# Conditioning rows of a hybrid decoder layer loaded as a stream of half rows, with the row rate set by stage

## The chip, the cores and the metric

The kernel runs on one core of a Trainium2 chip, as one program. The metric is the device time of one execution in microseconds (us). A core has TensorE (PE in the profile: matrix products into eight PSUM banks), VectorE (DVE), ScalarE (ACT), GpSimd (POOL) and SyncE (SP). SP does nothing here but issue DMA transfers, one after the other; each issue waits until the tile that it fills is free, and what stands behind it in SP's queue waits too.

## The reference, cut to what matters

One decoder layer on x (512 tokens by 2048), all in fp32. A conditioning vector c gives six modulation vectors of 2048 each, by a 2048 by 12288 matrix (100 MB, the largest input):

```python
c_act = jax.nn.silu(c)
mod = (c_act @ w_ada + b_ada).reshape(B, 6, D)
sh1, sc1, gt1, sh2, sc2, gt2 = [mod[:, j][:, None, :] for j in range(6)]

h = rmsnorm(x, g_norm_mix) * (1.0 + sc1) + sh1
q, k, v, xr, xg = split(h @ w_in)
o_attn = stick_breaking_attention(q, k, v)                 # 8 heads of 128
hr = rg_lru(causal_depthwise_conv(xr, w_conv, b_conv), ...)  # width 1024
o_lru = hr * gelu(xg)
mixed = concat([rmsnorm(o_attn, g_attn_out), rmsnorm(o_lru, g_lru_out)])
x = x + gt1 * (mixed @ w_out)

h = rmsnorm(x, g_norm_mlp) * (1.0 + sc2) + sh2
x = x + gt2 * (square(relu(h @ w_mlp_in)) @ w_mlp_out)
return rmsnorm(x, g_norm_final)
```

## The kernel before, in words

Tokens lie along the free axis, channels on the 128 partitions, so x is 16 blocks of 128 by 512. Every product is made three times: each operand is split into a rounded high part (ACT, a copy to fp32r) and the remainder (DVE, `low`, line 112), and `mm3` (lines 217 to 223) issues high x high, high x low, low x high.

A **row** of w_ada is the 2048 weights of 128 modulation values: 128 partitions by 2048, 1 MB. `ada` loads it in two halves of 512 KB into tiles with the tag `x` and multiplies each on DVE by the broadcast silu(c) (`cb`), which also sums along the row (line 178, STT below); line 185 adds the two sums and the bias. There are 96 rows, 16 for each of SC1, SH1, GT1, SC2, SH2 and GT2. GT2 has code of its own in the MLP, which the change leaves alone.

The work before the MLP, in the order of PE:

- **Phase 1** (the loop at `for k in range(NK)`): 16 steps of 24 products of 512 columns make the recurrence input xr from w_in and the *unnormalized* x times (1 + sc1) times the gain. Step k needs x block k, row k of SC1 (`prep1`) and 512 KB of w_in. The sum of squares of x runs beside it; a POOL all-reduce and six small operations (`rnorm`) turn it into r1.
- **Phase 2**: 16 steps for the first two heads' q and k and four heads' v. Step k needs row k of SH1 and the normalized block k (`prep2`: t = x r1, high and remainder of t + sh1).
- **q and k of heads 2 to 7, v of heads 4 to 7, xg**: `qk_group(2)`, `v_group(4)`, `qk_group(4)`, `qk_group(6)`, `xg_group(0)`, `xg_group(4)`, 16 steps (ticks) of 12 products each. Attention (`pair`), the recurrence (`conv`, `gates`, `scans`) and the rows of GT1, SC2, SH2 (`adas`) are put between them by lanes: a lane yields a number of ticks to wait before its next piece. For rows that number is `pace[0]`.
- **Out product**: 48 ticks of w_out, rows beside them at pace 1.58 and 1.42, until SH2 is done (`ensure`).

Loads of weights go into `wr` tiles (four of them) at raised priority; `later` pins an instruction to the place in its queue where the code has it. Pools: `x` had three tiles of 1024 columns, `tt` five of 1280 (temporaries of attention, and of the squares in phase 1).

## Time and profile before

| | |
|---|---|
| time, median of 3 runs | 2094.67 us (2091.67 to 2095.12) |
| the profiled execution, its own time | 2092.94 us |
| its span, first to last instruction | 2091.2 us |
| PE busy | 2016.1 us, 96% of the span |
| DVE busy | 1765.3 us, 84% |
| ACT busy | 1084.4 us, 52% |
| DMA | 441.46 MB, mean 211 GB/s |

A matrix product's busy time overlaps the next one's, so 96% is not a measure of how close PE is to its best; stages are compared by how long they take for the same number of products. Rows in the views have the start in us, the duration, engine, line, operation and tiles, and in brackets the idle time of the engine before it and what ended it. A line of waits gives the total, the number and the longest.

### The profile page before, as it was taken

Reading aid. Unit: us, or ns where it says so; the run is one execution under the profiler, and the core shown is the slowest. Engines: PE = TensorE matmul, PEld = TensorE weight load, DVE = VectorE, ACT = ScalarE, POOL = GpSimd, SP = SyncE. Lnnn points to the kernel's source line nnn. Section 1 sums busy time; section 2 is a strip of 40 time slices with the busy share of each in tenths; the row PEclk is TensorE's granted clock in tenths of the full one; section 3 lists DMA queues with packets and bytes.
Section 4 is the critical chain, followed back from the end, with each engine's and each line's share of the span. In section 5 each row is a group of like instructions: output and inputs, shape, how many; then the busy total and the mean of one; then the engine's idle time right before and its main releaser. Section 6 shows DMA issues by size and latency. Waiting matters only on the chain.

```text
span 2091.2 us, 38025 instructions
## 1 busy us (share of the span) xinstructions
PE 2016.1 (96%) x14532; PEld 1892.5 (90%) x14532; DVE 1765.3 (84%) x2993; ACT 1084.4 (52%) x1580; POOL 179.5 (9%) x282
## 2 busy tenths in 40 slices
PE   7989999999999898999999999999999999999997
PEld 5779898778777798999999999999999999999996
DVE  6898875878887679999999999999879778777986
ACT  4433564786432367555555545556435555555542
POOL 0000000000000000111211211200010210210000
PEclk9999999999999999999999999999999999999999
DMA  8887744535679743665655655655577667567744
GB/s 293 288 289 240 221 152 136 181 126 177 223 241 315 267 147 111 215 195 188 215 187 172 217 185 172 228 169 205 194 249 264 223 242 272 203 243 258 249 146 147
DMA packets 205625, 441.46 MB, mean 211 GB/s; under 512 B 20353, under 2 KB 41985, under 8 KB 205442
## 3 DMA queue, kind: packets, MB, share of 16 engines
q1 hardware_dynamic: 178642, 360.78, 52.2%
q0 software_dynamic: 21760, 71.32, 9.2%
q10 hardware_dynamic: 5040, 6.93, 1.0%
q8 instruction: 114, 1.87, 0.4%
q14 instruction: 69, 0.57, 0.1%
HBM read 375.25 MB, written 63.70 MB: 210 GB/s over the span
## 4 chain that ended last, share of the span: by engine, by line
PE 49%; DVE 3%; DMA 2%; issue 1%; ACT 0%; SPq 0%; DVEq 0%; ACTq 0%
PE ps_mm L1004 8%; PE ps_mm L1003 8%; PE ps_mm L1005 8%; PE ps_z L1004 6%; PE ps_z L1003 6%; PE ps_z L1005 6%; PE ps_o L1005 2%; PE ps_o L1004 2%; PE ps_o L1003 2%; DVE w L112 1%; DMA raw<-in_w_mlp_out_dram 1%; DMA a<-in_w_adaT_dram 1%; DMA a<-x 1%; DMA a<-sum 0%; DVE a L1180 0%
## 5 line engine op out<-in xcount | busy, mean ns | idle before, releaser
L1005 PE MATMUL ps_mm<-a,w 128*128 128x256 f32 x1696 | 476.6, 282 | 1.1 <-DVE w L112 1.1
L1003 PE MATMUL ps_mm<-a,w 128*128 128x256 f32 x1696 | 477.1, 282 | 0.5 <-DVE a L1016 0.5
L1004 PE MATMUL ps_mm<-a,w 128*128 128x256 f32 x1696 | 477.2, 282 | 0.0
L967 ACT ACTIVATE w<-raw 128x768 fp32r<-128x768 f32 x244 | 205.0, 841 | 330.8 <-PE ps_mm L1004 145.9
L1005 PE MATMUL ps_z<-a,w 128*128 128x256 f32 x1304 | 368.7, 283 | 7.0 <-DVE w L112 6.9
L112 DVE TENSOR_TENSOR w<-ts,w 128x1024 fp32r<-128x1024 f32 x244 | 297.7, 1220 | 89.5 <-PE ps_mm L1004 41.0
L1003 PE MATMUL ps_z<-a,w 128*128 128x256 f32 x1304 | 368.5, 283 | 0.5 <-DVE a L1019 0.5
L1004 PE MATMUL ps_z<-a,w 128*128 128x256 f32 x1304 | 368.3, 283 | 0.0
L973 ACT ACTIVATE w<-ts 128x1024 fp32r<-128x1024 f32 x244 | 258.3, 1059 | 152.1 <-DVE ts L969 134.2
L1005 PEld LDWEIGHTS ps_mm<-a,w 128*128 128x128 f32 x1696 | 319.3, 189 | 1.4 <-DVE w L112 1.4
L1003 PEld LDWEIGHTS ps_mm<-a,w 128*128 128x128 f32 x1696 | 319.4, 188 | 0.8 <-issue 0.7
L1004 PEld LDWEIGHTS ps_mm<-a,w 128*128 128x128 f32 x1696 | 319.6, 189 | 0.1
L112 DVE TENSOR_TENSOR w<-raw,w 128x768 fp32r<-128x768 f32 (+1 forms) x296 | 267.3, 904 | 42.7 <-ACT w L204 27.8
L1005 PEld LDWEIGHTS ps_z<-a,w 128*128 128x128 f32 x1304 | 246.8, 189 | 8.3 <-DVE w L112 8.2
L178 DVE SCALAR_TENSOR_TENSOR x<-x,cb 128x1024 f32<-128x1024 f32 x160 | 196.4, 1233 | 61.1 <-DMA x<-in_w_adaT_dram 60.5
L1003 PEld LDWEIGHTS ps_z<-a,w 128*128 128x128 f32 x1304 | 246.9, 189 | 0.9 <-issue 0.7
L1004 PEld LDWEIGHTS ps_z<-a,w 128*128 128x128 f32 x1304 | 246.9, 189 | 0.2 <-DVE a L112 0.2
L204 ACT ACTIVATE wh<-wr 128x512 fp32r<-128x512 f32 (+1 forms) x184 | 113.1, 618 | 171.3 <-PE ps_mm L222 74.3
L223 PE MATMUL ps_mm<-a,wl 128*128 128x512 f32 x448 | 178.0, 398 | 7.2 <-DVE wl L112 7.1
L219 PE MATMUL ps_mm<-a,wh 128*128 128x512 f32 x448 | 178.0, 397 | 4.0 <-DVE a L380 3.1
L222 PE MATMUL ps_mm<-a,wh 128*128 128x512 f32 x448 | 176.8, 395 | 0.0
L961 DVE TENSOR_TENSOR ts<-raw 128x512 f32<-128x512 f32 x244 | 166.5, 683 | 4.8 <-DMA raw<-in_w_mlp_out_dram 3.2
(326 smaller groups left out, 4087.0 us busy)
## 6 DMA issues: line engine op xcount, KB each, us to landing
x<-in_w_adaT_dram SPq DMA_DIRECT2D x160, 512.0 KB, 5.2
raw<-in_w_mlp_out_dram SPq DMA_DIRECT2D x124, 512.0 KB, 4.2
raw<-in_w_mlp_in_dram SPq DMA_DIRECT2D x120, 512.0 KB, 3.8
wr<-in_w_in_dram SPq DMA_DIRECT2D x160, 256.0 KB, 3.7
part<-a POOLq DMA_DIRECT2D x84, 256.0 KB, 3.7
a<-part SPq DMA_DIRECT2D x84, 256.0 KB, 6.1
prod<-a POOLq DMA_DIRECT2D x63, 256.0 KB, 6.2
sum<-a POOLq DMA_DIRECT2D x56, 256.0 KB, 3.7
```

The source lines that it names most:

```text
L112: tt(out=out, in0=full, in1=f32(high), op=ALU.subtract)
L178: stt(out=t, in0=t, scalar=1.0, in1=cb[q * n // 1024][:, o : o + n], op0=ALU.mult, op1=ALU.mult, accum_out=ga[:, q : q + 1],)
L204: act(h[:, :n], r[:, :n], AF.Copy)
L219: first = mm(out, wh, ah, start=start, stop=False, **kw)
L222: mm(out, wh, al, start=False, stop=False, **kw)
L223: mm(out, wl, ah, start=False, stop=stop, **kw)
L961: tt(out=t[:, : 2 * HT].rearrange("p (a b) -> p a b", a=2), in0=r[:, HT : 3 * HT].rearrange("p (a b) -> p a b", a=2), in1=r[:, q_(0)].unsq ...
L967: act(h, r[:, HT:], AF.Copy)
L973: act(h, t, AF.Copy)
L1003: mm(out, wh[:, blk(i)], ah, start=st, stop=False, **kw)
L1004: mm(out, wh[:, blk(i)], al, start=False, stop=False, **kw)
L1005: mm(out, wl[:, blk(i)], ah, start=False, stop=j == js[-1], **kw)
```

## The change

Four edits, all ahead of the MLP.

1. `ada` becomes `Rows`: a list of half rows in the order of use, `load(n, tags)` that issues the next n loads, and `row` that multiplies. In phases 1 and 2 (EARLY) the tiles come from `x` and `tt` in turn, each multiplication is followed by one more load, and a load more is made at each fourth step. GT1, SC2 and SH2 are loaded through `x` alone as they are used (MID) until `xg_group(4)`; from there five halves are loaded ahead through `x` and `tt` (LATE), each half has its own turn in the lane, and its multiplication is pinned. `x` has four tiles now, `tt` four.
2. The attention constants are made after phase 1 (`triangles`), by POOL and ACT; DVE no longer makes them at the start.
3. `prep1` splits straight from x: one ACT copy with the scale for the high part, one DVE operation for the remainder, in place of a scaled copy, a copy and a subtraction. x stays unscaled, so `prep2` multiplies by the gain as well.
4. x is loaded two blocks ahead and not three, the all-reduce is begun at step 13 and the small operations on r1 are written behind row 15; weights of step k + 1 are written ahead of step k's products. Row pace: 3.2 ticks instead of 3.5, 1.6 in the first half of `qk_group(4)`, 2.1 in the out product instead of 1.58 and 1.42.

```diff
-    "front": {"x": 3, "tt": 5, "wr": 4, "wh": 3, "wl": 3},
+    "front": {"x": 4, "tt": 4, "wr": 4, "wh": 3, "wl": 3},
...
+    class Rows:
+        def __init__(self, *ms):
+            self.todo = [(m * NK + j, q) for m in ms for j in range(NK) for q in range(2)]
+            self.tiles = {}
+        def load(self, n, tags):
...
+            for _ in range(n):
+                if self.todo and tags:
+                    i, q = self.todo.pop(0)
+                    t = T(next(tags))[:, :1024]
+                    later(queue.dma_start(t, w_adaT[i * P : (i + 1) * P, q * 1024 : (q + 1) * 1024]))
+                    self.tiles[i, q] = t
+        def row(self, m, j, tags, q=None):
...
+            for q_ in (0, 1) if q is None else (q,):
+                if (i, q_) not in self.tiles:
+                    self.load(2, tags)
+                t = self.tiles.pop((i, q_))
+                ins = stt(
+                    out=t, in0=t, scalar=1.0, in1=cb[q_], op0=ALU.mult, op1=ALU.mult, accum_out=self.ga[:, q_ : q_ + 1],
+                )
+                if q is not None:
+                    later(ins)
+                del t
+                if tags is not MID:
+                    self.load(1, tags)
...
+    rows, rows2 = Rows(SC1, SH1), Rows(GT1, SC2, SH2)
+    MID = itertools.cycle(["x"])
+    LATE = itertools.cycle(["x", "tt"])
...
-        act(xs[k], xs[k], AF.Identity, scale=g)
-        xhl[k] = split(xs[k], "a")
+        h, lo = T("a", F32R), T("a", F32R)
+        act(h, xs[k], AF.Copy, scale=g)
+        stt(out=lo, in0=xs[k], scalar=g, in1=f32(h), op0=ALU.mult, op1=ALU.subtract)
+        xhl[k] = h, lo
...
-        tt(out=t, in0=t, in1=r1, op=ALU.mult)
+        stt(out=t, in0=t, scalar=gm1[:, k : k + 1], in1=r1, op0=ALU.mult, op1=ALU.mult)
...
+    EARLY = itertools.cycle(["x", "tt"] * 3 + ["x"])
...
     for k in range(NK):
-        w = weights1(k)
...
         if k + 1 < NK:
-            prep1(k + 1)
-        if k >= NK - 2:
-            prep2(k - (NK - 2))
+            w_next = weights1(k + 1)
+            if k + 2 < NK:
+                load_x(k + 2)
+            if k + 2 == NK - 1:
+                r1_gen = rnorm_steps([acc], D, None)
+                next(r1_gen)
+            prep1(k + 1, EARLY)
+            if k + 1 == NK - 1:
+                r1 = next(r1_gen)
+            if k % 4 == 4 - 1:
+                rows.load(1, EARLY)
+        else:
+            prep2(0)
+            prep2(1)
...
+    triangles()
...
-    pace = [3.5]
+    pace = [3.2]
...
+    pace[0] = 1.6
+    def recurrence():
+        pace[0] = 3.2
...
+    tags2[0] = LATE
+    rows2.load(5, LATE)
     xg_group(4, BANKS[4:])
...
-    pace[0] = 1.58
+    pace[0] = 2.1
...
-    pace[0] = 1.42
+    pace[0] = 2.1
```

How this stands in the queues, at three places. **DVE at the start of the program**, before (`x_25` and `x_26` are the halves of SC1's row 0, `cb_1` and `cb_2` the halves of silu(c), `n_8` and `n_9` the constants):

```order
L134 MEMSET ones_64 128x128
L136 MEMSET n_8_88 128x128
L147 MEMSET eps_68 128x1
L142 CAST nones_r_66<-n_8_88 128x128
L446 TENSOR_SCALAR spl_72<-vec_63 128x8
L141 CAST ntri_65<-n_9_90 128x128
L178 SCALAR_TENSOR_TENSOR x_25_123,ga_24_122<-x_25_123,cb_1_76 128x1024
L178 SCALAR_TENSOR_TENSOR x_26_126,ga_24_122<-x_26_126,cb_2_77 128x1024
L185 SCALAR_TENSOR_TENSOR mods_69<-ga_24_122,vec_63 128x1
L317 SCALAR_TENSOR_TENSOR gm1_70<-mods_69,vec_63 128x1
```

and with the change (`x_20` and `tt_21` are the halves now):

```order
L148 MEMSET ones_64 128x128
L149 MEMSET eps_68 128x1
L492 TENSOR_SCALAR spl_72<-vec_63 128x8
L194 SCALAR_TENSOR_TENSOR x_20_108,ga_27_122<-x_20_108,cb_1_76 128x1024
L194 SCALAR_TENSOR_TENSOR tt_21_110,ga_27_122<-tt_21_110,cb_2_77 128x1024
L203 SCALAR_TENSOR_TENSOR mods_69<-ga_27_122,vec_63 128x1
L350 SCALAR_TENSOR_TENSOR gm1_70<-mods_69,vec_63 128x1
```

The constant `ntri`, which waits for POOL, stood ahead of the first row and is gone from DVE.

**DVE at the end of phase 1**, before, from SC1's row 15 (`x_222`, `x_223`) to the weights of phase 2 (`wl_265`); `n_208` and `n_209` are r1 in the making, `a_204` to `a_220` remainders of x blocks and of weights:

```order
L178 SCALAR_TENSOR_TENSOR x_222_933,ga_221_932<-x_222_933,cb_1_76 128x1024
L112 TENSOR_TENSOR a_214_894<-a_182_763,a_213_892 128x512
L178 SCALAR_TENSOR_TENSOR x_223_936,ga_221_932<-x_223_936,cb_2_77 128x1024
L289 TENSOR_SCALAR n_208_873<-n_208_873 128x512
L112 TENSOR_TENSOR a_217_923<-wr_215_920,a_216_922 128x512
L291 TENSOR_TENSOR n_208_873<-n_208_873,n_209_875 128x512
L112 TENSOR_TENSOR a_220_929<-wr_218_926,a_219_928 128x512
L292 SCALAR_TENSOR_TENSOR n_208_873<-n_208_873,n_209_875 128x512
L185 SCALAR_TENSOR_TENSOR mods_69<-ga_221_932,vec_63 128x1
L293 SCALAR_TENSOR_TENSOR n_209_875<-n_208_873,n_209_875 128x512
L317 SCALAR_TENSOR_TENSOR gm1_70<-mods_69,vec_63 128x1
L178 SCALAR_TENSOR_TENSOR x_227_947,ga_226_946<-x_227_947,cb_1_76 128x1024
L178 SCALAR_TENSOR_TENSOR x_228_950,ga_226_946<-x_228_950,cb_2_77 128x1024
L112 TENSOR_TENSOR wl_265_1072<-wr_263_1069,wh_264_1071 128x512
```

and with the change, from the square of x block 15 that the all-reduce waits for (`n_11`) to the first operation on r1 (`n_217`); `x_220` and `x_230` are halves of SH1's row 1, `tt_219` the second half of its row 0, `a_233` the remainder of x block 15:

```order
L353 SCALAR_TENSOR_TENSOR a_222_883<-a_202_812,gm1_70,a_221_882 128x512
L332 TENSOR_TENSOR n_11_99<-n_11_99,n_216_868 128x512
L194 SCALAR_TENSOR_TENSOR tt_219_875,ga_235_966<-tt_219_875,cb_2_77 128x1024
L203 SCALAR_TENSOR_TENSOR mods_69<-ga_235_966,vec_63 128x1
L194 SCALAR_TENSOR_TENSOR x_220_878,ga_240_979<-x_220_878,cb_1_76 128x1024
L112 TENSOR_TENSOR a_225_913<-wr_223_910,a_224_912 128x512
L112 TENSOR_TENSOR a_228_919<-wr_226_916,a_227_918 128x512
L353 SCALAR_TENSOR_TENSOR a_233_932<-a_215_866,gm1_70,a_232_931 128x512
L112 TENSOR_TENSOR wl_270_1066<-wr_268_1063,wh_269_1065 128x512
L112 TENSOR_TENSOR wl_273_1084<-wr_271_1081,wh_272_1083 128x512
L194 SCALAR_TENSOR_TENSOR x_230_924,ga_240_979<-x_230_924,cb_2_77 128x1024
L318 TENSOR_SCALAR n_217_871<-n_217_871 128x512
```

The operations on r1 stood between the last row, the weights' remainders and the closing of row 15; they now stand behind everything that phase 1 needs, and behind two weights of phase 2 and three halves of SH1.

**SP at the beginning of the out product**, before (`x` are half rows, `wr` weights of w_out):

```order
L196 DMA wr_1068_5290<-in_w_out_dram 128x512
L174 DMA x_1073_5317<-in_w_adaT_dram 128x1024
L174 DMA x_1074_5320<-in_w_adaT_dram 128x1024
L196 DMA wr_1075_5324<-in_w_out_dram 128x512
L196 DMA wr_1079_5346<-in_w_out_dram 128x512
L174 DMA x_1084_5369<-in_w_adaT_dram 128x1024
L196 DMA wr_1086_5376<-in_w_out_dram 128x512
L174 DMA x_1085_5372<-in_w_adaT_dram 128x1024
L196 DMA wr_1093_5406<-in_w_out_dram 128x512
L174 DMA x_1091_5399<-in_w_adaT_dram 128x1024
L174 DMA x_1092_5402<-in_w_adaT_dram 128x1024
```

and with the change:

```order
L219 DMA wr_1087_5320<-in_w_out_dram 128x512
L182 DMA x_1068_5278<-in_w_adaT_dram 128x1024
L219 DMA wr_1091_5346<-in_w_out_dram 128x512
L182 DMA tt_1073_5301<-in_w_adaT_dram 128x1024
L182 DMA x_1095_5369<-in_w_adaT_dram 128x1024
L219 DMA wr_1096_5372<-in_w_out_dram 128x512
L182 DMA tt_1101_5396<-in_w_adaT_dram 128x1024
L219 DMA wr_1102_5398<-in_w_out_dram 128x512
L182 DMA x_1106_5421<-in_w_adaT_dram 128x1024
L219 DMA wr_1107_5424<-in_w_out_dram 128x512
L219 DMA wr_1114_5455<-in_w_out_dram 128x512
```

Halves often came two next to each other; now one stands between two weights, in `x` and `tt` in turn, and five halves are loaded before the first of them is multiplied. Counted over SP's queue, the half rows are 10, 8, 20, 8 and 50 in `v_group(4)`, `qk_group(4)`, `qk_group(6)` with `xg_group(0)`, `xg_group(4)` and the out product before, and 12, 10, 25, 11 and 38 with the change. Ahead of the remainder of hT block 0 (the first operand of phase 2), DVE has 35 multiplications of half rows before and 38 with the change.

## Rows read from the trace of the kernel before

**Rows 1.** Windows by stage: busy us of each engine (count), PE clock, DMA share, GB/s.

```profile
15.77:123.51 107.74, 94.39 (x384) 73.86 (x385) 93.06 (x178) 50.82 (x86) 3.25 (x1) 0.97 0.87 299
123.51:213.97 90.46, 90.46 (x577) 81.93 (x576) 80.46 (x144) 32.74 (x52) 0.00 (x0) 1.00 0.77 257
334.86:386.58 51.72, 50.78 (x216) 40.34 (x216) 27.30 (x48) 28.33 (x47) 0.00 (x0) 1.00 0.44 139
386.58:513.23 126.65, 122.73 (x584) 101.19 (x585) 107.10 (x185) 92.70 (x139) 0.00 (x0) 1.00 0.49 158
558.20:706.95 148.75, 138.75 (x577) 106.72 (x575) 122.20 (x224) 46.00 (x77) 9.99 (x11) 1.00 0.82 280
```

**Rows 2.** Timeline of the start, ACT, DVE and PE.

```profile
7.73 1.06 ACT L153 ACTIVATE cb<-cb 128x1024 f32<-128x1024 f32 x1 [5.22 <-DMA cb<-in_c_dram]
...
10.75 0.23 DVE L141 CAST ntri<-n 128x128 fp32r<-128x128 f32 x1 [6.51 <-POOL n L138]
10.89 1.22 DVE L178 SCALAR_TENSOR_TENSOR x<-x,cb 128x1024 f32<-128x1024 f32 x1
...
15.77 0.80 PE L219 MATMUL ps_mm<-a,a 128*128 128x512 f32 x1 [7.92 <-ACT a L204]
```

**Rows 3.** Window from DVE's first half row to the first operand of phase 2.

```profile
10.85:115.10 104.25, 87.20 (x360) 68.16 (x360) 89.84 (x173) 49.51 (x84) 3.25 (x1) 0.99 0.85 293
```

**Rows 4.** Waits of DVE, 8 to 124 us.

```profile
DVE x L178 <- DMA x<-in_w_adaT_dram: 7.8, 11, 1.8
...
DVE n L301 <- ACT tt L300: 4.9, 7, 1.4
```

**Rows 5.** Groups of DVE, 10.5 to 123.5 us: busy us, mean ns of one.

```profile
L112 DVE TENSOR_TENSOR a<-a,a 128x512 fp32r<-128x512 f32 x16 | 11.0, 685 | 0.3 <-ACT a L116 0.3
...
L185 DVE SCALAR_TENSOR_TENSOR mods<-ga,vec 128x1 f32<-128x1 f32 x18 | 3.8, 213 | 0.1
```

**Rows 6.** Timeline of the end of phase 1, DVE and POOL.

```profile
98.90 3.28 DVE L178 SCALAR_TENSOR_TENSOR x<-x,cb 128x1024 f32<-128x1024 f32 x1 [0.18 <-DMA x<-in_w_adaT_dram]
...
114.31 0.75 DVE L327 SCALAR_TENSOR_TENSOR a<-a,mods,a 128x512 fp32r<-128x512 f32 x1
...
121.28 1.28 DVE L334 COPY a<-ps_mm 128x512 f32<-128x512 f32 x2
...
98.86 3.25 POOL L280 PARTITION_ALL_REDUCE n<-n  x1 [88.15 <-DVE n L301]
```

**Rows 7.** Timeline of PE, 109 to 124 us.

```profile
109.61 0.39 PE L223 MATMUL ps_o<-a,a 128*128 128x512 f32 x1
116.32 0.80 PE L219 MATMUL ps_mm<-a,a 128*128 128x512 f32 x1 [6.32 <-ACT a L204]
...
116.91 0.63 PE L222 MATMUL ps_mm<-a,a 128*128 128x512 f32 x1
117.34 0.63 PE L223 MATMUL ps_mm<-a,a 128*128 128x512 f32 x1
...
123.28 0.40 PE L223 MATMUL ps_o<-a,a 128*128 128x512 f32 x1
123.51 0.40 PE L219 MATMUL ps_mm<-a,wh 128*128 128x512 f32 x1
```

**Rows 8.** Waits of PE, then of DVE, in the out product.

```profile
PE ps_mm L223 <- DVE wl L112: 7.1, 8, 1.9
PE ps_z L223 <- DVE wl L112: 2.5, 4, 1.5
...
DVE x L178 <- DMA x<-in_w_adaT_dram: 26.7, 23, 3.4
```

**Rows 9.** The multiplications of half rows in the out product: shortest, median, longest ns.

```profile
L178 DVE SCALAR_TENSOR_TENSOR x<-x,cb x48: 1211/1224/1227, 557.4 to 702.7; 128x1024 f32<-128x1024 f32 x48
```

**Rows 10.** Timeline of ACT in the second pair of heads.

```profile
305.69 1.27 ACT L564 ACTIVATE tt<-tt 128x1280 fp32r<-128x1280 f32 x1 [0.54 <-DVE tt L562]
...
309.34 0.60 ACT L597 ACTIVATE a<-ps_o 128x512 f32<-128x512 f32 x1 [1.34 <-PE ps_o L223]
```

More of the change, by code (lines that the diff above doesn't have):

```diff
@@ L263, in tick, with group @@
             lane.run(dt)
-    def group(banks, ks, src, operand, halfway=None):
+    def group(banks, ks, src, operand, begun=(0, None)):
         for i, k in enumerate(ks):
-            if i == len(ks) // 2 and halfway:
-                halfway()
+            if i == begun[0] and begun[1]:
+                begun[1]()
             wh, wl = weights(src(k))
@@ L336, in hybrid_layer_kernel, with weights1 @@
     AHEAD, XPRI = 3, 42
-    def weights1(k):
-        return [weights(w_in[blk(k), XR + i * 512 : XR + (i + 1) * 512], tag="a", urgent=min(k * 28, URGENT), pin=True) for i in range(2)]
+    def weights1(k, halves=(0, 1)):
+        return [weights(w_in[blk(k), XR + i * 512 : XR + (i + 1) * 512], tag="a", urgent=min(k * 28, URGENT), pin=True) for i in halves]
+    EARLY = itertools.cycle(["x", "tt"] * 3 + ["x"])
     banks = [bank(t) for t in BANKS]
+    rows.load(2, EARLY)
     load_x(0)
-    prep1(0)
-    for k in range(NK):
-        w = weights1(k)
-        if k == 0:
-            load_x(1)
-            load_x(2)
-        if k + AHEAD < NK:
-            load_x(k + AHEAD)
-        if k + AHEAD == NK:
-            r1 = rnorm([acc], D, None)
-        if k + 1 < NK:
-            prep1(k + 1)
-        if k >= NK - 2:
-            prep2(k - (NK - 2))
+    w = weights1(0, [0])
+    prep1(0, None)
+    w += weights1(0, [1])
+    load_x(1)
+    rows.load(2, EARLY)
+    for k in range(NK):
+        if k + 1 < NK:
+            w_next = weights1(k + 1)
[12 more added lines that the diff above has]
+            prep2(1)
         for hf in range(2):
@@ L360, in hybrid_layer_kernel @@
                 mm3(banks[hf * 4 + o], wh[:, blk(o)], wl[:, blk(o)], *xhl[k], k == 0, k == NK - 1)
+        w = w_next
     xr_t = []
@@ L417, in hybrid_layer_kernel, with qk_group @@
     v_evac(banks[6:8], 2)
-    def qk_group(h0, halfway=None):
+    def qk_group(h0, begun=(0, None)):
         bs = [bank("mm") for _ in range(4)]
-        group(bs, range(NK), lambda k: src_qk[blk(k), :, h0 * P : (h0 + 2) * P], lambda k: hT[k], halfway)
+        group(bs, range(NK), lambda k: src_qk[blk(k), :, h0 * P : (h0 + 2) * P], lambda k: hT[k], begun)
         qk_evac(bs, h0)
@@ L620, in adas @@
         for j in range(NK):
-            ada(m, j, "a" if m == GT2 else "x", True)
-            yield pace[0]
+            if tags2[0] is MID:
+                rows2.row(m, j, MID)
+                yield pace[0]
+            else:
+                for q in range(2):
+                    rows2.row(m, j, LATE, q)
+                    yield pace[0] / 2
         ready.add(m)
-    pace = [3.5]
+    pace = [3.2]
     def ensure(m):
@@ L667, in hybrid_layer_kernel @@
     bg.drain()
-    qk_group(4, lambda: bgl.add(*[gates(o) for o in range(4)], scans(range(4)), *[conv(o) for o in range(4, 8)]))
+    pace[0] = 1.6
+    def recurrence():
+        pace[0] = 3.2
+        bgl.add(*[gates(o) for o in range(4)], scans(range(4)), *[conv(o) for o in range(4, 8)])
+    qk_group(4, (8, recurrence))
     bg.add(pair(4))
-    qk_group(6, lambda: bgl.add(*[gates(o) for o in range(4, 8)], scans(range(4, 8))))
+    qk_group(6, (8, lambda: bgl.add(*[gates(o) for o in range(4, 8)], scans(range(4, 8)))))
     bg.drain()
```

86 lines of the change are left out of this document (42 added, 44 removed).

## The prediction

> **What bounds the kernel now.** I read the windows by stage first, then the waits in the two stages that stand out, then the timeline at their edges. PE is busy in nearly every stage, so a stage must be held against PE's best pace. Phase 2 is that pace: PE is busy in all of its 90.46 us [rows 1], and its 16 steps of 12 products of 512 columns and 24 of 256 are 196,608 columns, 0.460 ns each. Phase 1 has the same number of columns (384 products of 512) and takes 107.74 us, from a start at 15.77 [rows 1, 2]: 17 us over. The out product has 576 products of 512, 135.7 us at that pace, and takes 148.75 [rows 1]: 13 over. `qk_group(4)` has PE busy in 50.78 of 51.72 us and nothing to give [rows 1]. The MLP isn't touched. So there are two places where a change ahead of the MLP can earn, and what they wait for decides.
>
> In phase 1 it is DVE. From its first half row at 10.89 until the first operand of phase 2 is made (the remainder at 114.31, 0.75 us) DVE is busy 89.84 of 104.25 us; 7.8 of its idle time ends with a half row landing and 4.9 with ACT's square of an x block, which ACT makes late [rows 2 to 4, 6]. PE stands still for 6.32 us before the last step of phase 1 and runs it at half speed: 0.43 us from product to product at 116.91, against 0.23 at the end of the step [rows 7].
>
> In the out product DVE is busy 122.20 us, and its idle 26.55 us are the 26.7 us for which it waited 23 times for a half row [rows 1, 8]. DVE takes its queue in order, so a weight's remainder behind a half row that hasn't landed is late too: the waits of PE listed there, 9.6 us in 12, are for these remainders [rows 8]. The cause is the rows' loads, not DVE's work.
>
> **The change part by part.** *The start.* The cast of `ntri` held DVE until 10.75; silu of the first half of c is done at 7.73 + 1.06 = 8.79 [rows 2]. Without the cast the first half row is multiplied at 8.8, if it has landed; the second half of c is ready before it is wanted. DVE starts 2.1 us earlier.
>
> *DVE's work until phase 2 can begin.* The queue shows 38 half rows instead of 35, so 3 x 1.22 us [rows 9], two more closings of a row at 0.21 [rows 5], and two more normalized blocks at 0.75. The 16 remainders of x become the kind of the operation at 114.31, 0.75 instead of 0.685 [rows 5, 6]: 1.0. Together 6.6, so 89.84 + 6.6 = 96.4 us of work. The idle 14.4 us [rows 3] are the unknown. If every wait for rows and squares goes, 1.7 stay; if none, 14.4. Seven tiles in place of three let rows land two steps ahead, and ACT makes its square in front of the scaled copy now, but DMA share was 0.85 already and three halves more must come by then [rows 3]; I take 7, the middle. The all-reduce stays in it: a multiplication beside it took 3.28 us instead of 1.22 [rows 6, 9], and the queue has such a multiplication behind it again. DVE has the first operand at 8.8 + 96.4 + 7 = 112.2 (106.9 to 119.6).
>
> On this the Trainium skill (SBUF — State Buffer, Who interferes with whom) says that a VectorE instruction with two SBUF inputs and a GpSimd instruction that reads SBUF lock each other out, whoever starts first holding the ports to its end. The row agrees: 3.28 us against an all-reduce of 3.25. By the rule the instruction could lose the whole 3.25 and not 2.06, and the time would be 1.2 us more than the sum below.
>
> *The beginning of phase 2.* Its first bank must be emptied by DVE, behind one half row (1.22), one remainder (0.75) and with one copy (0.64, half of the pair at 121.28) [rows 6, 9]: 114.8. Step 15 of phase 1 doesn't decide any more: its remainder stands sixteen operations, some 12 us by their kinds, ahead of that of phase 2's first operand, so PE has done it by 107 and waits about 8 us. I charge the slow clock for this wait as for that of before: the last step took 116.32 to 123.51, 7.2 us, and 24 products at 0.23 are 5.5 [rows 7], so 1.7. Phase 2 is as if begun at 116.5, before at 123.51: **7.0 us gained**, with the bounds of the idle time 12.3 gained to 0.4 lost. Phase 2 has DVE busy 80.46 of 90.46 us and the same work per step, so it stays PE's.
>
> *The out product.* SP's queue has 38 half rows there in place of 50, one between two weights and five ahead. If the waits per half row stayed as they were, 12/50 of the 13 us would go, 3; if PE got the pace of phase 2, 13. Loads ahead are just what DVE's 26.7 us lacked, and the last halves stand well before the stage's end; against it, each multiplication is pinned. **9 us gained**, two thirds of the way.
>
> *Rows moved earlier.* 12 half rows, 14.7 us of DVE [rows 9], go to the stages of attention, recurrence and xg. Five of them come into 386.58 to 513.23, where DVE is busy 107.10 of 126.65 us [rows 1]; it becomes 113. In `qk_group(4)`, where the pace is 1.6, DVE is busy 27.30 of 51.72 and DMA at a share of 0.44 [rows 1], so the burst is covered by idle engines. DVE has room in the mean but not at each chain of a head; **2 us lost** (0 to 7, half of the moved time).
>
> *Four `tt` tiles for five.* The high part of the second head's logarithms (305.69) must now wait until the first head's values are read, where the copy of them starts at 309.34 [rows 10]: 3.7 us for ACT. The remainder behind it had to wait for a tile anyway, and PE has products of the group in that time. 0 us (0 to 3.7). The constants on POOL and ACT, x two blocks ahead and the saved scaled copy of ACT lie beside DVE's work: nothing.
>
> **Sum.** The profiled execution took 2092.94 us by its own clock, 1.7 more than its span and 1.7 less than the median of the runs shown, 2094.67. -7.0 - 9 + 2 = -14.0, so 2078.9 for such an execution and **2080.7** on the scale of the median. All bounds together reach from 25 gained to 8 lost.
>
> **Rivals.** *DVE keeps its idle time* (phase 1 is bound by rows arriving at 0.85 of DMA, however many tiles there are): 0.4 - 9 + 2, 2088. For it: x, weights and rows share one queue, and weights still wait for DVE to free `wr` tiles. Against it: phase 2 takes its half rows through the same queue at a DMA share of 0.77, and PE waits for nothing there [rows 1].
>
> *Moved work eats the gain*: the out product gives only its share of fewer rows, 3, and the moved rows cost 7 in the attention stages: -7 - 3 + 7, 2091.7.
>
> *The stream doesn't run ahead*: a load waits in SP's queue for a `wr` tile that DVE frees late, and the tiles ahead stand empty. Then both stages stay as they are: 2094.7.
>
> *Slower*: pinned multiplications in the out product. 43 halves are multiplied there, and DVE's other work with them is 122.2 - 5 x 1.22 = 116.1 us. If each half is waited for as those 23 were, 1.16 us in the mean, that is 50 us idle; the stage takes 166 us and not 148.75, and 17.3 - 7 + 2 makes 2107. It turns slower once the idle time passes 42 us, 1 us for each half. Against it: five halves are some five ticks at the new pace, about 14 us.
>
> **How the numbers follow.** A measurement of this kernel tells about 0.2%, 4.2 us, from no change: faster is under 2090.5, slower over 2098.9. The forecast, with 8 to 25 us gained, has 0.62; phase 1 unmoved 0.14; moved work eating the gain 0.10, half of it this side of 2090.5; no stream 0.08; slower 0.06. Faster is 0.62 + 0.14 + 0.05 = 0.81, same 0.13, slower 0.06. The range 2069 to 2093 goes from all bounds at their best to beyond the third case and leaves out the slower case, most of the fourth and a remainder below, together under 0.2.
>
> **What the profile of the change would show.** DVE's first half row at 8.8 and PE's first product about 3 us before 15.77. DVE's waits for rows in phase 1 well under 7.8, the first product of phase 2 at 113 to 116 after a pause of PE, phase 2 again 90 to 91 us. The out product at 138 to 142 us with DVE's waits for half rows under 8 us. 386.58 to 513.23 as long as before or 2 us longer. Wrong would be: DVE still idle 14 us in phase 1, an out product near 148, or attention stages that grow by more than 5.

## The result, and the profile after

The changed kernel takes **2065.79 us** in the median of five runs (2059.55 to 2067.12), the kernel before 2094.67 (2088.11 to 2095.86): ratio 0.9863, 95% interval 0.9841 to 0.9885, **28.9 us faster**. The direction was right, the size more than twice the forecast 14, and the time lies below the range. The profiled execution is the fastest of the five (span 2057.8 us against 2091.2), so the two profiles differ by 33.4 us.

Windows by stage of the changed kernel (phase 1, phase 2, the stretch of `qk_group(6)` and `xg_group(0)`, the out product; columns as in [rows 1]):

```profile
core 0: us, PE busy (x) PEld busy (x) DVE busy (x) ACT busy (x) POOL busy (x), PEclk, DMA share, GB/s
11.80:102.00 90.20, 90.09 (x384) 73.39 (x384) 88.22 (x169) 41.16 (x68) 4.94 (x3) 1.00 0.93 343
109.05:202.80 93.75, 92.95 (x577) 83.42 (x577) 81.09 (x142) 33.55 (x54) 0.00 (x0) 0.96 0.70 239
376.63:502.87 126.24, 122.84 (x584) 101.34 (x585) 106.64 (x187) 92.93 (x138) 0.41 (x1) 1.00 0.53 172
547.50:681.20 133.70, 133.68 (x575) 108.00 (x574) 110.25 (x200) 44.50 (x74) 8.52 (x10) 1.00 0.77 268
```

Phase 1, here up to its last product, has PE busy in 90.09 of 90.20 us and DVE in 88.22: both engines have lost nearly all their idle time, and DMA moves 343 GB/s at a share of 0.93. Phase 2 begins at 109.05 and not at 123.51, ends 11.2 us earlier (202.80 against 213.97), but is itself 3.3 us longer, at a granted clock of 0.96. The out product takes 133.70 us and not 148.75, PE never idle.

DVE's waits up to phase 2, answering to [rows 4]:

```profile
DVE x L194 <- DMA x<-in_w_adaT_dram: 5.8, 2, 4.7
DVE a L353 <- ACT a L352: 0.8, 4, 0.2
DVE a L112 <- ACT a L227: 0.4, 1, 0.4
DVE tt L194 <- DMA tt<-in_w_adaT_dram: 0.4, 1, 0.4
```

Of the 5.8 us for half rows 4.7 stand ahead of the very first one, at 7.73; the waits inside phase 1, 7.8 and 4.9 before, are gone.

DVE's timeline at the end of phase 1 with POOL's all-reduce, then ACT's and PE's at the beginning of phase 2 (idle time before in brackets):

```profile
90.81 4.11 POOL L306 PARTITION_ALL_REDUCE n<-n  x1 [80.09 <-DVE n L332]
...
91.85 2.07 DVE L203 SCALAR_TENSOR_TENSOR mods<-ga,vec 128x1 f32<-128x1 f32 x1
93.84 1.21 DVE L194 SCALAR_TENSOR_TENSOR x<-x,cb 128x1024 f32<-128x1024 f32 x1
...
100.37 0.68 DVE L322 TENSOR_TENSOR n<-n,n 128x512 f32<-128x512 f32 x1
101.44 1.23 DVE L194 SCALAR_TENSOR_TENSOR tt<-tt,cb 128x1024 f32<-128x1024 f32 x1 [0.40 <-DMA tt<-in_w_adaT_dram]
102.59 0.08 DVE L194 DVE_READ_ACCUMULATOR tt<-tt,cb 128x1 f32 x1
102.59 0.69 DVE L323 SCALAR_TENSOR_TENSOR n<-n,n 128x512 f32<-128x512 f32 x1
104.41 1.23 DVE L194 SCALAR_TENSOR_TENSOR x<-x,cb 128x1024 f32<-128x1024 f32 x1 [1.13 <-DMA x<-in_w_adaT_dram]
105.56 0.08 DVE L194 DVE_READ_ACCUMULATOR x<-x,cb 128x1 f32 x1
105.56 0.69 DVE L324 SCALAR_TENSOR_TENSOR n<-n,n 128x512 f32<-128x512 f32 x1
106.16 0.21 DVE L203 SCALAR_TENSOR_TENSOR mods<-ga,vec 128x1 f32<-128x1 f32 x1
106.29 2.07 DVE L359 SCALAR_TENSOR_TENSOR a<-a,gm,n 128x512 f32<-128x512 f32 x3
```

```profile
107.13 1.38 ACT L361 ACTIVATE a<-a,mods 128x512 fp32r<-128x512 f32 x2 [7.10 <-DVE a L359]
108.42 1.06 ACT L367 ACTIVATE a<-ps_mm 128x512 f32<-128x512 f32 x2
...
101.52 0.39 PE L246 MATMUL ps_o<-a,a 128*128 128x512 f32 x1
109.05 0.79 PE L242 MATMUL ps_mm<-a,wh 128*128 128x512 f32 x1 [7.15 <-ACT a L367]
109.65 0.63 PE L245 MATMUL ps_mm<-a,wh 128*128 128x512 f32 x1
110.07 0.63 PE L246 MATMUL ps_mm<-a,wl 128*128 128x512 f32 x1
111.49 0.80 PE L242 MATMUL ps_mm<-a,wh 128*128 128x512 f32 x1 [0.79 <-DVE a L369]
```

Between the operations on r1 (lines 322 to 324) stand two half rows of SH1's *third* row, which have not landed: DVE waits 0.40 and 1.13 us and then multiplies for 1.2 us each. The first normalized block (line 359) comes behind them, ACT's operations on it (line 361) behind that, and ACT's copies that empty the banks (line 367) last. PE stands still for 7.15 us until the first of these copies is done. Then its products follow each other at 0.6 and 0.42 us instead of 0.23, which is the slow clock, and it waits 0.79 us more for DVE to empty the second bank. So of the 3.3 us that phase 2 is longer, 0.8 are this wait and 2.5 the clock.

### The profile page after: what moved, and what is told of

It reads as the page before. It is cut to its first block, busy times and chain, and to the rows that moved or that the text cites. A ratio compares the mean times of both kernels' runs of the same rounds, so it can differ in the third digit from the quotient of the medians.

```text
span 2057.8 us, 37989 instructions
## 1 busy us (share of the span) xinstructions
PE 2004.1 (97%) x14532; PEld 1891.8 (92%) x14532; DVE 1767.7 (86%) x2990; ACT 1078.5 (52%) x1568; POOL 180.1 (9%) x283
## 5 line engine op out<-in xcount | busy, mean ns | idle before, releaser
L112 DVE TENSOR_TENSOR wl<-wr,wh 128x512 fp32r<-128x512 f32 (+1 forms) x184 | 125.0, 681 | 45.2 <-ACT wh L227 44.0
```

The lines of the kernel that those rows point to most:

```text
L112: tt(out=out, in0=full, in1=f32(high), op=ALU.subtract)
```

## The experiments

Every run is timed beside the kernel before on the same chip. "Begins" and "ends" are the starts of the first product of phase 2 and of the stage behind it; "attention" is the time from that end to the out product, "out" from there to the first product of the MLP, all from one profile.

| kernel | median us | ratio to before, 95% | phase 2 begins | ends | attention | out |
|---|---|---|---|---|---|---|
| before | 2094.67 | | 123.51 | 213.97 | 344.2 | 151.0 |
| before, second profile | 2092.27 | 0.9996 (0.9975 to 1.0016) | 123.41 | 213.87 | 348.7 | 150.4 |
| changed | 2065.79 | 0.9863 (0.9841 to 0.9885) | 109.05 | 202.80 | 344.7 | 137.0 |
| changed, second time | 2063.58 | 0.9853 (0.9831 to 0.9874) | 108.38 | 202.50 | 345.2 | 136.6 |
| early part alone | 2085.47 | 0.9959 (0.9942 to 0.9976) | 109.26 | 202.74 | 352.4 | 152.0 |
| late part alone | 2076.97 | 0.9922 (0.9896 to 0.9948) | 125.28 | 215.74 | 351.3 | 137.4 |
| new pace, no late stream | 2077.44 | 0.9919 (0.9893 to 0.9945) | 109.19 | 203.77 | 343.0 | 146.3 |
| late stream, old pace | 2068.10 | 0.9877 (0.9853 to 0.9900) | 107.97 | 202.62 | 353.1 | 136.6 |
| early stream shallow | 2061.88 | 0.9844 (0.9821 to 0.9868) | 107.59 | 201.32 | 343.5 | 138.3 |
| the same, three x tiles | 2066.59 | 0.9867 (0.9845 to 0.9889) | 108.57 | 203.72 | 350.8 | 138.3 |
| constants first | 2063.10 | 0.9855 (0.9832 to 0.9878) | 109.08 | 201.91 | 347.3 | 136.9 |
| old split | 2064.69 | 0.9860 (0.9835 to 0.9886) | 111.30 | 205.01 | 343.7 | 137.7 |
| x three ahead | 2061.54 | 0.9839 (0.9820 to 0.9859) | 109.00 | 202.92 | 347.1 | 136.6 |
| weights in their step | 2064.60 | 0.9849 (0.9829 to 0.9868) | 107.65 | 202.76 | 345.0 | 137.9 |
| rows not pinned | 2060.99 | 0.9835 (0.9815 to 0.9855) | 107.39 | 201.31 | 344.0 | 137.2 |
| four of these undone | 2073.19 | 0.9897 (0.9872 to 0.9923) | 116.62 | 211.55 | 344.8 | 137.5 |
| early: stream alone | 2070.50 | 0.9888 (0.9862 to 0.9914) | 118.08 | 208.54 | 344.5 | 137.2 |
| before, four x tiles | 2095.05 | 1.0004 (0.9988 to 1.0020) | 125.32 | 215.78 | 354.6 | 150.1 |
| r1 first | **2055.90** | **0.9819 (0.9796 to 0.9842)** | 104.65 | 195.38 | 344.1 | 138.7 |
| r1 first, rows ahead all along | 2059.63 | 0.9835 (0.9812 to 0.9857) | 104.24 | 196.95 | 343.3 | 137.6 |

### Controls: what one profile is worth

The changed kernel again.

> The changed kernel itself a second time, as the control for the sums of stages: what differs between its two profiles is chance. Theory (the stages from 203 to 548 us, where a half row that lands late can stand ahead of a bank's evacuation, vary by some 5 to 9 us from execution to execution, and the stages of the MLP by 1 to 4 with the places where the clock falls): the whole 2060 to 2067 us, phase 2's end within 1 us of 202.8, the out product within 1.5 us of 137.0 to the first product of the MLP. Rival (executions are alike, and stage lengths of one profile are the kernel's): every stage within 0.5 us.

The rival held ahead of the MLP: the stages of the two profiles differ by 0.6 us at most. In the MLP they do vary, 1359.4 and 1363.3 us from its first product to its last.

The kernel before again.

> The kernel before itself, profiled a second time. Theory (as the two profiles of the changed kernel agree within 0.6 us in every stage ahead of the MLP, stage lengths are the kernel's own): phase 2 ends at 213 to 215 us, the stages from there to the out product take 343 to 346 us. Rival (with three x tiles and the old paces a half row lands now ahead of, now behind a bank's evacuation): 348 to 355 us, and the kernel before varies by its attention stages.

Neither expectation held: phase 2's end agrees within 0.1 us, attention takes 348.7 us, between the two expectations (with a slow clock of 3.4 us at 277.3 that the first profile lacks). So attention stages of the kernel before are known to some 5 us, and phase 2's end to some 2: the late part alone (below), whose code up to there is that of the kernel before, ends it 1.8 us later than the first profile. A profile also shows one execution, which can lie far from the median of its kernel: 10.2 us over it with the late part alone, 6.1 with four x tiles in the kernel before, 4.8 with the early part alone, 2.1 with the shallow stream and three x tiles, and 6 under it with the new pace alone and in the first profile of the changed kernel. What one profile says of a long stage has to be held against the medians.

### Early and late, stream and pace

Early part alone:

```diff
-    pace = [3.2]
+    pace = [3.5]
...
-    pace[0] = 1.6
...
-    tags2[0] = LATE
-    rows2.load(5, LATE)
...
-    pace[0] = 2.1
+    pace[0] = 1.58
...
-    pace[0] = 2.1
+    pace[0] = 1.42
```

> The change with its late part undone: rows of GT1, SC2, SH2 through x tiles alone as they are used, row paces 3.5, 1.58 and 1.42 as before. Theory (two separate gains, phase 1 and the out product, that add up): phase 2 ends at about 203 us instead of 213.97 as in the changed kernel, the out product takes 146 to 150 us again with DVE waiting 20 us or more for half rows, the whole is 10 to 13 us faster than before, 2082 to 2085 (ratio 0.994 to 0.995). Rival 1 (the early gain is eaten later, because attention and recurrence follow their own chain): the stages from 214 to 558 grow by the same 11 us, 2094. Rival 2 (the first loops of the MLP got faster through the early part or by chance of the clock): they take 96.7 and 47.6 us as in the changed kernel; by the theory that they follow the out product they take 100.8 and 49.1 as before.

Late part alone, in the kernel before (with all the new paces, of which one is shown):

```diff
             else:
                 for q in range(2):
+                    rows2.row(m, j, LATE, q)
+                    yield pace[0] / 2
...
+    tags2[0] = LATE
+    rows2.load(5, LATE)
...
-    pace[0] = 1.58
+    pace[0] = 2.1
```

> The kernel before with the late part alone: the stream of half rows for GT1, SC2, SH2 and the new paces; phases 1 and 2, the constants and the pools (3 x, 5 tt) as before. Theory: phase 2 ends at 214 as before, the out product takes 133 to 136 us instead of 148.75, and the whole is 13 to 18 us faster, 2077 to 2082 (ratio 0.991 to 0.994). Rival 1 (early and late gains are not separate: the stream needs the fourth x tile): 140 us or more, under 9 us gained. Rival 2 (the MLP's 4 to 8 us come from the late part): the first two loops of the MLP take 96.7 and 47.6 us here and 100.8 and 49.1 in the run with the early part alone.

New pace without the stream, and the stream at the old pace (with all the old paces, of which one is shown):

```diff
-    tags2[0] = LATE
-    rows2.load(5, LATE)
```

> The changed kernel with its stream of the late rows undone: the rows of GT1, SC2, SH2 go through x tiles alone, both halves of a row in one turn, with the new paces 3.2, 1.6 and 2.1. Theory of the prediction (the loads ahead give most of it; fewer rows alone give 12/50 of the 13 us over the best pace): out product 143 to 147 us, DVE waiting 15 us or more for half rows, 8 to 12 us slower than the changed kernel, 2075 to 2078. Rival (the pace alone does it, one row in 2.1 ticks leaves the loads time enough): out product 133 to 137 us, waits for half rows under 5 us, 2066 as the changed kernel.

```diff
-    pace[0] = 2.1
+    pace[0] = 1.58
```

> The changed kernel with the old row paces 3.5, 1.58 and 1.42: the same 50 half rows as before are left for the out product, but as a stream with five loads ahead. Theory (the loads ahead give most): out product 136 to 141 us, DVE's waits for half rows under 8 us, 2068 to 2073. Rival (the number of rows counts, since DVE and DMA have no room for 12 more): out product 144 to 150 us, 2076 to 2082.

The two gains add up: 9.4 us early and 17.9 late by the medians on their chip, and 28.9 for both. In the out product the stream does it: at the old pace, with all 50 half rows, it takes 136.6 us, at the new pace without the stream 146.3. Beside the stream the new pace shows nothing in the whole: 0.9877 (0.9853 to 0.9900) with the old one, 0.9863 (0.9841 to 0.9885) with the new. In the windows of the run with stream and old pace DVE is busier than in the changed kernel, and PE is still never idle:

```profile
555.71:689.00 133.29, 133.29 (x575) 108.10 (x574) 120.61 (x226) 44.35 (x74) 8.47 (x10) 1.00 0.85 303
```

The waits of DVE, then of PE, in the out product of the run with the new pace alone:

```profile
DVE x L194 <- DMA x<-in_w_adaT_dram: 20.4, 13, 5.1
```

```profile
PE ps_mm L246 <- DVE wl L112: 3.8, 8, 0.9
PE ps_z L246 <- DVE wl L112: 2.6, 3, 1.8
```

DVE waits for thirteen half rows, and PE for the remainders behind them, as in [rows 8].

In the profile of the early part alone the attention stages did what the rival said, for 8 of its 11 us: they take 352.4 us against 344.2. The medians say otherwise. Of the 11.2 us by which phase 2 ends earlier, 9.4 arrive at the end of the kernel, so some 2 are lost behind it, by the interval 6 at most; the rival's 2094 fell, and 2085.47 is close to the theory's 2082 to 2085. What such a loss is made of, DVE's and PE's timelines at the end of `v_group(4)` in that run show at one place:

```profile
320.48 0.68 DVE L112 TENSOR_TENSOR x<-a,x 128x512 fp32r<-128x512 f32 x1
325.12 1.23 DVE L194 SCALAR_TENSOR_TENSOR x<-x,cb 128x1024 f32<-128x1024 f32 x1 [3.96 <-DMA x<-in_w_adaT_dram]
...
326.88 1.88 DVE L444 TENSOR_TENSOR a<-ps_mm,a 128x512 fp32r<-128x512 f32 x3
```

```profile
327.61 0.79 PE L242 MATMUL ps_mm<-a,wh 128*128 128x512 f32 x1 [3.57 <-DVE a L444]
```

A half row that lands late stands ahead of the evacuation of the banks (line 444), and PE waits for the banks, 3.57 us. The next stage then begins at half clock (0.50 from 326.9 to 333.7).

### What made phase 1 faster

Single undos in the changed kernel. Shallow: x tiles alone, three halves ahead; and the same with three x tiles.

```diff
-    EARLY = itertools.cycle(["x", "tt"] * 3 + ["x"])
+    EARLY = itertools.cycle(["x"])
...
-    rows.load(2, EARLY)
+    rows.load(1, EARLY)
...
-            if k % 4 == 4 - 1:
-                rows.load(1, EARLY)
```

> The changed kernel with the early stream cut to x tiles alone and three half rows ahead (no tt tiles, no load more at each fourth step). Theory (phase 1's gain is the depth of the stream: DVE no longer finds a half row that hasn't landed): DVE waits 5 us or more for half rows in phase 1 (1.5 in the changed kernel), phase 2 ends at 206 to 210 us instead of 202.8, the whole 3 to 7 us slower than the changed kernel. Rival (depth is not needed, the gain comes from the earlier start and from the order of loads in the queue): phase 2 ends at 202 to 204, waits for half rows under 2.5 us, no difference.

> The run with the shallow early stream (x tiles alone, three halves ahead) with three x tiles instead of four, so that each load must wait for the multiplication just ahead of it, as in the kernel before. Theory (the fourth tile): SP waits 25 us or more for multiplications in phase 1, DVE waits 5 us or more for half rows, phase 2 ends at 206 to 211 against 201.3 with four tiles. Rival (the order of the loads in SP's queue): phase 2 ends at 201 to 203 with three tiles too.

Four x tiles in the kernel before:

```diff
-    "front": {"x": 3, "tt": 5, "wr": 4, "wh": 3, "wl": 3},
+    "front": {"x": 4, "tt": 4, "wr": 4, "wh": 3, "wl": 3},
```

> The kernel before with four x tiles and four tt tiles instead of three and five, and nothing else. In the kernel before SP's queue stands 28.9 us, 17 times, for a half row's tile that DVE is still multiplying, and everything behind in that queue stands too. Theory (phase 1's idle time came from the third x tile: a load is issued only when the half three before it is multiplied): these waits of SP fall under 10 us, DVE's waits for half rows in phase 1 from 7.8 to under 4, phase 2 ends at 206 to 211 instead of 213.97, the whole 3 to 8 us faster than before. Rival (it is the order in which loads stand in SP's queue, x three blocks ahead and row loads not pinned, not the tile): phase 2 ends at 213 to 215, no difference.

The rivals held up to 0.8 us: phase 2 ends at 201.32 (they had 202 to 204), 203.72 (201 to 203) and 215.78 (213 to 215). Depth and the fourth tile are not what phase 1 needed. In the last run SP's wait for a multiplication falls from 28.9 to 5.5 us and nothing is gained, as the wait only moves: SP then stands for weights' tiles that DVE frees (lines 317 and 112), 54.6 us and not 31.3. SP's waits in the kernel before, then with four x tiles:

```profile
SPq L174 <- DVE x L178: 28.9, 17, 7.1
SPq L196 <- DVE gm L317: 21.9, 11, 2.9
SPq L196 <- DVE a L112: 9.4, 14, 3.4
```

```profile
SPq L196 <- DVE gm L317: 35.8, 12, 4.6
SPq L196 <- DVE a L112: 18.8, 14, 7.2
SPq L174 <- DVE x L178: 5.5, 3, 4.3
```

Constants at the start, the old split, x three blocks ahead, a step's weights written in that step, row loads left to the scheduler:

```diff
+    nc.vector.tensor_copy(ntri, ntri_f)
+    nc.vector.tensor_copy(nones_r, nones)
...
-    triangles()
```

> The changed kernel with the attention constants made at the start as before, their casts on DVE. Theory (DVE is phase 1's bound, so what it starts late it ends late): DVE's first half row at 10.7 to 11 us instead of 7.7, phase 2 ends 2 to 3 us later than 202.8, the whole 2 to 3 us slower than the changed kernel. Rival (phase 1 is bound by DMA at a share of 0.93, so a later start of DVE is made good by rows that have landed meanwhile): phase 2 ends within 1 us of 202.8.

```diff
-        act(h, xs[k], AF.Copy, scale=g)
-        stt(out=lo, in0=xs[k], scalar=g, in1=f32(h), op0=ALU.mult, op1=ALU.subtract)
+        act(xs[k], xs[k], AF.Identity, scale=g)
+        xhl[k] = split(xs[k], "a")
...
-        stt(out=t, in0=t, scalar=gm1[:, k : k + 1], in1=r1, op0=ALU.mult, op1=ALU.mult)
+        tt(out=t, in0=t, in1=r1, op=ALU.mult)
```

> The changed kernel with the old way to split x (scaled copy on ACT, copy on ACT, subtraction on DVE; the normalized block by a plain multiplication). DVE has 1 us less work, ACT 10 us more. Theory (the split is worth nothing by itself): phase 2 ends within 1 us of 202.8, the whole within 3 us of the changed kernel. Rival (the two ACT copies in a row are what made ACT's squares late and DVE wait for them, 4.9 us before): DVE waits 3 us or more for ACT in phase 1, phase 2 ends at 205 to 208.

```diff
-                load_x(k + 2)
+                load_x(k + 3)
```

> The changed kernel with the blocks of x loaded three steps ahead, as before, instead of two. Theory (not a cause): phase 2 ends within 1 us of 202.8, or up to 1 us earlier as r1 is ready sooner. Rival (x three ahead takes DMA from the rows and makes ACT's squares stand in front of casts): DVE waits 3 us or more for rows or squares, phase 2 ends at 205 or later.

```diff
-            w_next = weights1(k + 1)
+                w = weights1(k)
```

> The changed kernel with the weights of a step written in that step, as before, and not one step ahead, so that DVE multiplies the next row ahead of this step's remainders of the weights. Theory (this order is what made PE wait: a late half row or square then holds the remainders that PE wants at once; the last step's weights stand behind the first rows of SH1): steps of phase 1 of over 5.6 us come back, above all the last two, phase 2 ends at 207 to 213 us instead of 202.8, the whole 4 to 9 us slower than the changed kernel. Rival (it doesn't matter): phase 2 ends within 1 us of 202.8.

```diff
-                    later(queue.dma_start(...))
+                    if tags is not EARLY:
+                        later(dma)
```

> The changed kernel with the early loads of half rows not pinned in SP's queue, so that the scheduler places them, as before. Theory (a small cause): phase 2 ends within 1.5 us of 202.8. Rival (pinning is what keeps half rows in time): DVE waits 4 us or more for half rows behind the first, phase 2 ends at 206 or later.

None gives back more than 2.2 us of phase 2's end, little more than the 1.8 that no edit explains. The old split gives back most, and DVE's waits for an ACT copy of x (line 116) come with it:

```profile
DVE a L112 <- ACT a L116: 4.2, 5, 0.9
```

With the constants first, PE's first product comes 1.7 us later (13.53), but phase 2 begins no later. The weights in their own step make steps 5 and 15 of phase 1 longer (7.18 and 6.09 us against 5.44), which the pause before phase 2 swallows. As the parts seemed to cover for one another, two runs undid several: constants, split, x and weights together; and then also the place of r1's operations.

```diff
-            if k + 2 == NK - 1:
-                r1_gen = rnorm_steps([acc], D, None)
-                next(r1_gen)
+            if k + 3 == NK:
+                r1 = rnorm([acc], D, None)
```

> The changed kernel with four of its early edits undone together: constants at the start, the old split, x three blocks ahead, weights written in their own step. The stream of half rows and the place of r1's operations stay. Theory (the parts cover for one another, so together they show what each hides: 2 us from the split, 3.6 us in steps 5 and 15 from the weights, 1.7 us from the start): phase 2 begins at 113 to 118 us, the whole 4 to 9 us slower than the changed kernel. Rival (the stream is enough): phase 2 begins at 107 to 111.

> The same with r1's operations and the first normalized block back at their old places, so that the stream of half rows alone is left of the early part. Theory (r1's place is what holds the tail of phase 1: steps 14 and 15 and the pause behind them take 20 us before): phase 2 begins at 117 to 122 us, 3 us or more later than with r1's operations at their new place. Rival (the stream alone does it): phase 2 begins at 107 to 112.

The theory held for the four: 8.7 us of phase 2's end go, where the four apart come to 1.4 (-0.9, 2.2, 0.1 and 0.0). It fell for r1: with its old place phase 2 begins 1.5 us later and *ends* 3 us earlier. PE doesn't pause between the phases (its first product, at 118.07, is one pitch behind the last of phase 1, at 117.84), where with the four undone it stands for 1.15 and then 2.57 us, and the clock stays up:

```profile
118.08:208.54 90.46, 90.46 (x578) 81.94 (x577) 81.21 (x143) 32.79 (x52) 0.00 (x0) 1.00 0.78 262
```

DVE's waits in phase 1 of the run with the stream alone:

```profile
DVE a L112 <- ACT a L116: 7.5, 9, 1.4
DVE x L192 <- DMA x<-in_w_adaT_dram: 3.9, 1, 3.9
```

The one wait for a half row is that of the start. So the stream takes away the waits for rows, and the long steps 14 and 15 are gone (7.65 and 12.88 us before, 5.57 and 5.44 here): phase 2 ends 5.4 us earlier, of which 1.8 are PE's earlier first product (13.98 for 15.77). The waits for ACT's squares, 4.9 us before [rows 4], are gone as well. But others come up in their place, for an ACT copy of x (line 116), 7.5 us where the kernel before has 0.3, and steps 2, 4, 5, 12 and 13 take 7.3 to 8.7 us, before 5.4 to 6.2. These go with the other edits: the remaining 5.7 us of phase 2's end, 9.0 by its beginning less 3.3 by its length. Which of the four edits does how much of it is not separated.

### The pause before phase 2

r1's operations, the first normalized block and the bank copies ahead of the third row of SH1:

```diff
+        with tc.high_priority(offset=first):
             act(r, r, AF.Exp, scale=-0.5)
             tt(out=m, in0=m, in1=r, op=ALU.mult)
...
-            prep2(1)
...
-        copy(o, t, banks[o])
+            later(copy(o, t, banks[o]))
         xr_t.append(t)
+    prep2(1)
```

> The changed kernel with another order on DVE between the phases: r1's operations, the first normalized blocks and the bank copies stand ahead of the two half rows of SH1's third row, for which DVE waits 1.5 us between r1's operations in the changed kernel. Nothing else is changed. Theory (PE's pause of 7.2 us before phase 2, and the slow clock behind it, come from this order alone): phase 2's first product at 103 to 104.5 us instead of 109.05, its end at 195 to 199 instead of 202.8, the whole 4 to 8 us faster than the changed kernel, 2058 to 2062. Rival (the postponed half rows are wanted at once, so the pause only moves into the first steps of phase 2): PE waits 3 us or more in 104 to 125, phase 2 ends at 201 to 204, no difference.

The theory held. PE's timeline at the edge, and the window of phase 2:

```profile
102.00 0.39 PE L246 MATMUL ps_o<-a,a 128*128 128x512 f32 x1
104.65 0.50 PE L242 MATMUL ps_mm<-a,wh 128*128 128x512 f32 x1 [2.26 <-ACT a L370]
```

```profile
104.65:195.38 90.73, 90.53 (x576) 81.71 (x577) 83.94 (x148) 33.41 (x55) 0.00 (x0) 1.00 0.79 269
```

The pause is 2.26 us and not 7.15, the granted clock stays at 1.00, and phase 2 ends 7.4 us earlier: 4.4 by its beginning, 2.4 by the clock, 0.6 by less waiting of PE for the banks. Which of the three things moved ahead counts most was not separated. The median is 7.7 us under the changed kernel's second and 9.9 under its first; the three single undos timed with it on one chip take 2061.88 to 2064.69. It is the best version found.

Then rows ahead in the attention stages as well:

```diff
+    rows2.load(2, MID)
     bg2.add(adas(GT1), adas(SC2), adas(SH2))
```

> The kernel with r1's operations first, and with the rows of the attention stages also loaded ahead: two halves ahead through x tiles from v_group(4) on, one load behind each multiplication; three more halves ahead at the switch to the late stream. Theory (a half row that hasn't landed holds DVE's queue wherever it stands): DVE's waits for half rows from 195 to 540 us fall from 20 to under 8 us, the stages from phase 2's end to the out product take 341 to 344 us, the whole 1 to 4 us faster than with r1 first alone, 2052 to 2055. Rival (PE has no waits there that hang on rows, so nothing is to be had): within 1 us of 2055.9, or slower if loads held in SP's queue for an x tile delay weights.

The rival held: DVE's waits for half rows there stay (22.2 us against 21.0), attention is 0.8 us shorter, the whole is not faster. PE's pause before phase 2 is 2.74 us in this run, the granted clock is 0.50 from 105.6 to 109.0, and phase 2 takes 92.71 us instead of 90.73.

## Why the prediction was wrong in size

The table sets the prediction's own steps against the first pair of profiles, which differ by 33.4 us; its last row is what the others leave over.

| step | predicted us | measured us |
|---|---|---|
| beginning and speed of phase 2 | -7.0 | -11.2 |
| moved rows, attention | +2 | +0.5 |
| out product to the MLP | -9 | -14.1 |
| MLP | 0 | -8.6 |

**The idle time of phase 1** was mis-sized. DVE's work was well counted: 97.6 us from its first half row to the first operand of phase 2, against 96.4. Its idle time there is 3.7 us, against the 7 taken as "the middle" of 1.7 and 14.4. With the start at 7.73 and not 8.8, that operand is ready at 109.03 instead of 112.2. The reason given, tiles for rows "two steps ahead", was wrong as well: three halves ahead do the same. Nor did the start count: with the constants first phase 2 begins when it did. The rest of the reason, ACT's squares, fell in part: the stream alone removes the waits for them, and what the split and its companions remove are waits for an ACT copy that the stream alone brings up, which the prediction had at nothing.

**The beginning of phase 2.** The forecast put a half row, a remainder and a copy, 2.6 us, between operand and product, as DVE was to empty the bank. ACT emptied it: the first product began at 109.05, just as the remainder, which the second product needs, was ready. So phase 2 begins 5.75 us before the forecast 114.8. Against that phase 2 was 3.3 us longer, 2.5 by the slow clock behind the pause, for which 1.7 were charged, and 0.8 by the wait for the second bank; the sign given, phase 2 at "90 to 91 us", was wrong. The all-reduce held a closing of a row (2.07 us for 0.21, at 91.85), no multiplication. The Trainium skill (SBUF — State Buffer, Who interferes with whom) counts a VectorE operation with two SBUF inputs against a GpSimd instruction that reads SBUF, and has the port pair that they share as an exclusive lock. Here the closing finished at 93.9, and a multiplication of a half row took its usual 1.21 us from 93.84 on, while the all-reduce lasted to 94.9 by POOL's rough spans: the cost was 1.9 us, and no lock shows to the all-reduce's end. Nor does the row of the kernel before agree with it as fully as the prediction has it: the multiplication of 3.28 us ended at 102.18, 0.07 us behind the all-reduce, so it can't have stood until then and run its 1.22 us after.

**The out product** was mis-sized: "two thirds of the way" to a bound that was too slow. The bound came from phase 2's 0.460 ns per column, 135.7 us; the stage ran at 0.232 us per product of 512, which is 0.453 ns per column and 133.70 us. And the way is whole: no wait of DVE for half rows is left there. The mechanism, loads ahead and not fewer rows, was right, and so was the share of fewer rows: 3 us estimated, 4.7 measured.

**Moved rows** were put at 2 us lost and measured 0.5, less than the 4.5 us by which the two profiles of the kernel before differ, so the term is neither shown nor refuted. In the profiles, kernels with four x tiles at the old pace have attention stages of 352.4, 353.1 and 354.6 us, kernels with three x tiles at the new pace 350.8 and 351.3; four tiles at the new pace 343 to 347, three at the old 344.2 and 348.7. That changing either alone costs something is not shown by this: four of the five long ones are from executions over their kernel's median, and by the medians four x and four tt tiles alone show no cost (ratio 1.0004, 0.9988 to 1.0020). What the long ones share is that the granted clock falls to 0.50 within these stages; among the eleven profiles of the changed kernel and its variants with 343 to 346 us it does so in one. The one place shown is a half row ahead of a bank's evacuation; that the others are the same is not shown. The 0 us put down for four tt tiles stand in this; which of the two pools matters was not separated.

**"The MLP isn't touched"** holds for the code, and 8.6 us of the profile's difference lie there. The two profiles of before take 1368.0 and 1362.4 us from the MLP's first product to its last, the two of the changed kernel 1359.4 and 1363.3: a mean difference of 4, of the size of the scatter. About 2.2 us of it repeat in both pairs, in the MLP's first loop (28.85 and 28.86 against 26.56 and 26.72); but the kernel before with four x tiles has 26.67 too, so what shortens that loop is open. Nor do the halves settle it: the first two loops take 98.8 and 48.7 us with the early part alone, 98.4 and 47.7 with the late part alone, both between the kernel before (100.8 and 49.1) and the changed one (96.7 and 47.6). With 4 in place of 8.6 the steps add up to 28.8, the measured 28.9. The steps ahead of the MLP alone, 24.8 us by these profiles, would give 2069.9, just inside the range at 2069; so the mis-sized terms carried the time to the range's edge, and these 4 us, put at nothing and open in their cause, past it.

**The rivals** all fell: DVE did not keep its idle time, the stream ran ahead, and the pinned multiplications of the out product wait for nothing. That moved work eats the gain is false of this kernel, and of the early part alone too: its profile lost 8 of 11 us in the attention stages, its median some 2.

## What to carry to other kernels

Loads put ahead of an in-order queue pay where that queue waited for them, and where nothing else is late at the same place, a wait that is taken away counts whole; the prediction's "middle" was a guess that no row supported. Something else can be late: with the stream alone 7.5 us came back as waits for ACT. Then read the order at the edges of stages: an operation that waits for a transfer there holds everything behind it, and putting r1, the first block and the bank copies ahead of two half rows ended phase 2 7.4 us earlier, where no single undo of the early part cost more than 2.2. Hold a long stage of one profile against the medians before it is explained. Undo edits together as well as singly, since parts that cover for one another each look worthless.

## What the runs showed of the hardware

The clock at the edge of the phases in the changed kernel, in a window of its own:

```profile
105.40:115.60 10.20, 5.75 (x13) 4.07 (x14) 10.20 (x20) 4.22 (x8) 0.00 (x0) 0.50 0.95 376
```

It fell to its lower level, 1.2 GHz, while PE stood still in a pause of 7.15 us, and stayed there 6.5 us after PE had begun again; phase 2 was 3.3 us longer, 2.5 of it by the clock. With a pause of 2.26 us (r1 first) it did not fall there; with one of 2.74 (rows ahead all along) it fell behind the pause, for 3.4 us. A mean of 343 GB/s at a DMA share of 0.93 was held for 90 us by loads of 256 and 512 KB, more than the 293 of [rows 3].
